# Memory attention of the prompt: scores from two row halves into a bank per head, in place of padded keys

## The chip, the cores and the metric

One Trainium2 chip, and one of its cores. The time is the device time of one execution in microseconds (us): the median of three runs. The profile is of one execution more, taken by the hardware profiler. TensorE has two sequencer streams in it: PE are its matmuls, PEld the loads of its stationary operand. DVE is VectorE, ACT is ScalarE, POOL is GpSimd, and SP is SyncE, which issues most of the DMAs.

## The reference, cut to what matters

The program is one step of a decoder layer, for a prompt of 4096 tokens and for 8 sequences of 4 new tokens. All branches read one projection of the normalized input, 12 blocks of 256 columns. The branch of this change is the cross-attention of the prompt's tokens into 256 memory tokens, with 4 heads of 64:

```
mk, mv = jnp.split(mem @ w, 2, axis=-1)                   # (1, 256, 4, 64) each
def mem_attend(q, mk, mv):
    s = jnp.einsum("nlhd,nmhd->nhlm", q, mk) * (64 ** -0.5)
    p = jax.nn.softmax(s, axis=-1)
    return jnp.einsum("nhlm,nmhd->nlhd", p, mv)
```

Its result is normalized, gated and multiplied with the output projection together with the other three branches (a state space model, a short convolution, and a stick-breaking attention).

## The kernel before, in words

The program has two stages. The first (tile pools `sb1` and `ps1`, up to about 1960 us) goes through the prompt in 8 chunks of 512 tokens. For each chunk it multiplies 24 column blocks of 128 with the chunk's input (`proj`, lines 218 to 220: three fp32r matmuls of 512 columns for each of 8 slices, into the tile `pj`). After each quarter or half of a block, `between` and `slot` let other work into the order: they step generators in the list `bg` (memory attention, state space model, transposed stores, merges) and the decode's generator. This is an order written out by hand, and each engine runs its instructions in it. The second stage (lines 1380 and on) does the prompt's stick-breaking attention (`scores`, line 1449, tile `z`) and the output projection.

The memory attention of a chunk is `mem_gen`, once for each pair of heads (`hp`), so 16 times in all. It takes the four tiles of 128 tokens in two halves. `score` makes the scores of one tile of tokens: one fp32 matmul (line 789) whose stationary operand is `mq`, the transposed queries of both heads of the pair (64 rows each), and whose moving operand is `mkbd`. This holds the keys of both heads beside each other, 512 columns, with zeros where the rows of one head meet the columns of the other, so that one matmul over 128 rows gives the scores of both heads apart. An fp32 matmul stands in the trace as two passes. The result fills one PSUM bank, the tile `ms_`. VectorE takes the maximum of each head (line 791) and scales it (line 792); ScalarE computes the exponentials (the tile `p`; all activations have line 42) with this as bias. Exp needs another table than the activations around it, so an ACT_TABLE_LOAD stands ahead of the exponentials. `scale` divides by the sums (lines 773 and 775), `turn` transposes the weights (line 781, tile `pT`) and copies them out of PSUM, on VectorE for even tiles of tokens and on ScalarE for odd ones, and `mem_pv` multiplies with the values (line 821, tile `mo`).

Two calls of `score` always stand next to each other: tiles 0 and 1 at the start of `mem_gen`, and tiles 2 and 3 behind `mem_pv` of tile 0. So there are 32 such pairs, called score steps below: 16 first ones and 16 second ones. A second step stands right behind `turn(1)`, whose copy out of PSUM is ScalarE's, and `mem_pv(0)`.

The PSUM tiles of `ms_` come from `trp`, the tag `tr`, which has two banks. All transposes of the first stage share them (`pT`, `xx`, `ub`, `uT`, `yT`, `rt`, `bc`, `nat`, `xT`, `wT`, `cT`, `hT`): they are given out in turn, and the next user of a bank waits until the last instruction that reads the one before has ended. Behind a score step, the next user in the order of the program gets the bank of the step's first tile, and the one after it the other.

No two fp32 matmuls over 64 rows stand beside each other in this kernel. Column tiles are used in fp32 in stage one: lines 821 (64 columns of the array) and 1084 (16 columns, the decode's scores, tile `dz`). In stage two line 1449 multiplies over 64 rows, one head in each half of the array, in fp32r, one head's matmul next to the other's.

Of the kernel before, what the change touches and what calls it, by code (L numbers as in the profile page):

```python
# [8 lines left out]
F32 = mybir.dt.float32  # L9
F32R = mybir.dt.float32r  # L10
I32 = mybir.dt.int32
AF = mybir.ActivationFunctionType
ALU = mybir.AluOpType
AX = mybir.AxisListType
# [15 lines left out]
def hymba_kernel(ctx: ExitStack, tc: tile.TileContext, x_p, x_s, cache_k, cache_v, s_re, s_im, s_conv,  # L30
# [7 lines left out]
    mm, tr = nc.tensor.matmul, nc.tensor.transpose  # L38
    V, S, P, SP = nc.vector, nc.scalar, nc.gpsimd, nc.sync

    def act(out, in_, f=AF.Copy, **kw):
        return S.activation(out, in_, f, **kw)  # L42
# [68 lines left out]
    sb = p1.enter_context(tc.tile_pool(name="sb1", bufs=1))  # L111
# [3 lines left out]
    def ev(dt=F32, name="ev"):  # L115
        return sb.tile([128, 512], dt, tag="ev", name=name, bufs=5)

    def m4(name, shape=(128, 2, 512)):
        return sb.tile(list(shape), F32, tag="m4", name=name, bufs=5)

    def m8(name, shape=(128, 2, 1024)):
        return sb.tile(list(shape), F32, tag="m8", name=name, bufs=1)

    def trp(name="trp"):
        return ps.tile([128, 4, 128], F32, tag="tr", name=name, bufs=2)

    def msp(name="msp"):
        return ps.tile([128, 512], F32, tag="ms", name=name, bufs=2)
# [54 lines left out]
    def x_tile(name="xt", dt=F32):  # L183
        return sx.tile([128, DM], dt, tag="xt", name=name, bufs=4)
# [532 lines left out]
            yield  # L717


    mkbd = sb.tile([128, 2, 2, 256], F32, name="mkbd")  # L720
    mv = sb.tile([128, 2, GW], F32, name="mv")

    def mem_setup():
        mT = m8("mT", (128, KT, 256))
        xts, wms = [], {}
        for i in range(2):
            xts.append(x_tile())
            SP.dma_start(xts[i], mem_p[0, i * 128:(i + 1) * 128, :])

        def wm_load(cc):  # L730
            if cc < 4:
                wms[cc] = m4("wm", (128, KT, 128))
                SP.dma_start(wms[cc], w_mem[cc])
        V.memset(mkbd, 0.0)
        wm_load(0)
        wm_load(1)
        yield
        for i in range(2):
            for k4 in range(2):
                t = trp("mTp")  # L740
                for k in range(4):
                    tr(t[:, k, :], xts[i][:, (k4 * 4 + k) * 128:(k4 * 4 + k + 1) * 128], ident)
                V.tensor_copy(mT[:, k4 * 4:k4 * 4 + 4, i * 128:(i + 1) * 128], t)
            yield
        mk = m4("mk", (128, 2, 2, 256))
        for cc in range(4):
            wm = wms.pop(cc)
            wm_load(cc + 2)
            o = msp("mo")
            for i in range(2):  # L750
                for k in range(KT):
                    mm(o[:, i * 128:(i + 1) * 128], mT[:, k, i * 128:(i + 1) * 128], wm[:, k, :],
                       start=(k == 0), stop=(k == KT - 1))
            V.tensor_copy(mk[:, cc // 2, :, cc % 2 * 128:cc % 2 * 128 + 128],
                          o[:, 0:256].rearrange("p (i f) -> p i f", i=2))
            yield
        V.tensor_copy(mv, mk[:, 1])
        SP.dma_start(o_mk[0, 0].rearrange("(i p) h d -> p i (h d)", p=128), mk[:, 0])
        SP.dma_start(o_mv[0, 0].rearrange("(i p) h d -> p i (h d)", p=128), mk[:, 1])
        t = trp("mkT")  # L760
        for hp in range(2):
            for i in range(2):
                tr(t[:, 2 * hp + i, :], mk[:, 0, i, hp * 128:(hp + 1) * 128], ident)
        for hp in range(2):
            for h in range(2):
                V.tensor_copy(mkbd[h * 64:h * 64 + 64, hp, h, :].rearrange("p (i m) -> p i m", i=2),
                              t[h * 64:h * 64 + 64, 2 * hp:2 * hp + 2, :])

    def mem_gen(mq, Y, hp):
        pts, mxs = [], []  # L770

        def scale(t):
            V.reciprocal(mxs[t][:, 6:8], mxs[t][:, 4:6])
            for h in range(2):
                V.tensor_scalar(pts[t][:, h, :], pts[t][:, h, :], mxs[t][:, 6 + h:7 + h], None, op0=ALU.mult)

        def turn(t):
            tp = trp("pT")
            for h in range(2):
                for m in range(2):  # L780
                    tr(tp[:, 2 * h + m, :], pts[t][:, h, m * 128:(m + 1) * 128], ident)
            pT = ev()
            (act if t % 2 else V.tensor_copy)(pT, tp.rearrange("p a b -> p (a b)"))
            return pT

        def score(t):
            s = trp("ms_")
            s2 = s.rearrange("p a b -> p (a b)")
            mm(s2, mq[:, t * 128:(t + 1) * 128], mkbd[:, hp].rearrange("p h m -> p (h m)"), start=True, stop=True)
            mx = sb.tile([128, 8], F32, tag="mx", name="mx", bufs=4)  # L790
            V.tensor_reduce(mx[:, 0:2], s2.rearrange("p (h m) -> p h m", h=2), axis=AX.X, op=ALU.max)
            V.tensor_scalar(mx[:, 2:4], mx[:, 0:2], -0.125, None, op0=ALU.mult)
            p = sb.tile([128, 2, 256], F32, tag="q4", name="p", bufs=4)
            for h in range(2):
                act(p[:, h, :], s2[:, h * 256:(h + 1) * 256], AF.Exp, scale=0.125, bias=mx[:, 2 + h:3 + h],
                    accum_out=mx[:, 4 + h:5 + h])
            pts.append(p)
            mxs.append(mx)
        score(0)
        score(1)  # L800
        yield
        o = msp("mo")
        for t in (0, 2):
            scale(t)
            scale(t + 1)
            yield
            pT = turn(t)
            yield
            pT2 = turn(t + 1)
            mem_pv(o, pT, t, hp)  # L810
            if t == 0:
                score(2)
                score(3)
            yield
            mem_pv(o, pT2, t + 1, hp)
        act(Y[:, hp, :], o)

    def mem_pv(o, pT, t, hp):
        for m in range(2):
            for h in range(2):  # L820
                mm(o[h * 64:h * 64 + 64, t * 128:(t + 1) * 128],
                   mv[:, m, (2 * hp + h) * 64:(2 * hp + h) * 64 + 64],
                   pT[:, (2 * h + m) * 128:(2 * h + m) * 128 + 128], start=(m == 0), stop=(m == 1))
# [383 lines left out]
    def post(i):  # L1207
# [25 lines left out]
        elif blk == M_Q:  # L1233
            mq = sb.tile([128, 512], F32, tag="mq", name="mq", bufs=2)
            act(mq, o)
            if ft == 0:
# [4 lines left out]
                st["mem"] = []  # L1241
                bg.append(chain(st["mem"]))
            st["mem"].append(mem_gen(mq, st["Ym"], ft))
        elif blk == B_C:
            conv_c(o, ft, c)
# [48 lines left out]
    bg.append(dec_consts())  # L1294
    setup = ssm_setup()
    mset = mem_setup()

    def first():
# [8 lines left out]
    i = 0  # L1307
    while i < len(seq):
        c, k = divmod(i, npc)
# [58 lines left out]
    sb = ctx.enter_context(tc.tile_pool(name="sb2", bufs=1, reuse_waits="tile"))  # L1368
# [505 lines left out]
    for i in range(nu + LAG + 1):  # L1874
        j = i - LAG
        z = None
        if i < nu:
            qc, hp, kb, qt = units[i]
# [64 lines left out]
```

## Time and profile before

| | us |
|---|---|
| median of 3 runs | 3415.83 |
| lowest and highest run | 3399.83, 3421.22 |
| profiled execution | 3414.53 |
| its span, first to last instruction | 3412.8 |
| mean granted TensorE clock | 0.973 of full speed |

The profiled execution is 1.3 us below the median. The trace has PE busy in 93% of the span, DVE in 67%, ACT in 52% and POOL in 37%. A busy PE is not PE at its peak, since a matmul's record holds its latency too: what it costs in a row of matmuls is read from start to start.

### The profile page before, as it was taken

How to read it: one execution, taken by the hardware profiler on the slowest of the kernel's cores; microseconds unless marked ns; L12 is line 12 of the kernel's file. 1: busy time of each engine (PE TensorE's matmuls, PEld its weight loads, DVE VectorE, ACT ScalarE, POOL GpSimd, SP SyncE). 2: the span in 40 equal slices, each digit the busy share in tenths (PEclk: the TensorE clock that was granted, in tenths of full speed). 3: DMA queues.
4: the chain of work that ended last, by engine and by line, in shares of the span. 5: the costliest groups of instructions: out<-in, count | busy, mean ns of one | idle time of the engine just before them, and what ended most of it. 6: DMA issues, size and time to landing. Idle time of an engine off the chain costs nothing. (4 is left out here: it accounts for less than half of the span.)

```text
span 3412.8 us, 65273 instructions
## 1 busy us (share of the span) xinstructions
PE 3164.8 (93%) x23383; PEld 2282.1 (67%) x23383; DVE 2283.0 (67%) x3628; ACT 1780.8 (52%) x3324; POOL 1267.6 (37%) x1721
## 2 busy tenths in 40 slices
PE   7888999999999999999999988998999888999998
PEld 6556767667677677676676655666666555666667
DVE  5875667666676676676756566667666777677773
ACT  3435544443444444444434366666656666667771
POOL 1465322222231122222222045555545445555560
PEclk9899999999999999999999979999999999999999
DMA  6677887888877878878887443232323223222223
GB/s 212 194 209 224 279 268 238 264 279 274 267 251 254 286 245 290 263 234 277 270 262 214 142 163 103 91 97 87 97 87 95 71 91 102 94 86 75 88 66 117
DMA packets 382179, 623.57 MB, mean 183 GB/s; under 512 B 54568, under 2 KB 245488, under 8 KB 381856
## 3 DMA queue, kind: packets, MB, share of 16 engines
q1 hardware_dynamic: 344912, 484.90, 45.1%
q0 software_dynamic: 36944, 134.50, 11.9%
q8 instruction: 186, 3.05, 0.4%
q14 instruction: 137, 1.12, 0.1%
HBM read 539.33 MB, written 79.95 MB: 181 GB/s over the span
## 5 line engine op out<-in xcount | busy, mean ns | idle before, releaser
L45 POOL TENSOR_TENSOR bt<-bt,T 128x512 f32<-128x512 f32 (+3 forms) x576 | 605.9, 1052 | 632.2 <-DVE T L1470 417.0
L218 PE MATMUL pj<-xh,whl 128*128 128x512 f32 (+1 forms) x1792 | 724.9, 405 | 0.0
L1470 DVE TENSOR_TENSOR_SCAN T<-om,cy,z 128x513 f32<-128x513 f32 x448 | 549.7, 1268 | 249.3 <-ACT bt L42 96.6
L220 PE MATMUL pj<-xh,whl 128*128 128x512 f32 (+1 forms) x1792 | 658.7, 368 | 9.4 <-DVE whl L45 9.4
L219 PE MATMUL pj<-xh,whl 128*128 128x512 f32 (+1 forms) x1792 | 658.2, 367 | 0.1
L888 POOL DMA_INDIRECT kt<-in_cache_sb_k_dram,idxk x256 | 298.4, 1166 | 898.5 <-DVE kT L1056 787.0
L42 ACT ACTIVATE wT<-wt 128x512 f32<-128x512 f32 (+3 forms) x360 | 194.5, 556 | 448.8 <-PE wt L1487 448.2
L218 PEld LDWEIGHTS pj<-xh,whl 128*128 128x128 f32 x1792 | 344.3, 192 | 120.2 <-issue 82.0
L220 PEld LDWEIGHTS pj<-xh,whl 128*128 128x128 f32 x1792 | 344.0, 192 | 70.3 <-DVE whl L45 12.3
L42 ACT ACTIVATE bt<-z,b 128x512 f32<-128x512 f32 (+3 forms) x576 | 385.2, 669 | 0.0
L42 ACT ACTIVATE om<-z,nb 128x512 f32<-128x512 f32 (+3 forms) x576 | 380.4, 660 | 2.8 <-PE z L1453 2.8
L219 PEld LDWEIGHTS pj<-xh,whl 128*128 128x128 f32 x1792 | 345.6, 193 | 44.9 <-issue 8.6
L1487 PE MATMUL wt<-ident,bt 128*128 128x128 f32 x2112 | 299.5, 281 | 35.2 <-DVE Yc L45 13.5
L1056 DVE STREAM_TRANSPOSE kT<-kt 128x1024 f32<-128x1024 f32 x256 | 315.3, 1232 | 14.9 <-DMA kt<-in_cache_sb_k_dram,idxk 10.3
L1449 PE MATMUL z<-kst,qst 64*128 64x512 f32 (+3 forms) x1704 | 300.1, 424 | 24.2 <-DVE T L1470 21.7
L1487 PEld LDWEIGHTS wt<-ident,bt 128*128 128x128 f32 x2112 | 241.4, 143 | 105.4 <-issue 59.0
L45 DVE TENSOR_TENSOR whl<-stg,whl 128x1024 fp32r<-128x1024 f32 x191 | 234.1, 1226 | 109.3 <-ACT whl L42 99.0
L1503 PE MATMUL ya<-wT,vt 128*64 128x256 f32 (+1 forms) x2176 | 262.8, 382 | 0.3 <-DVE wT L1490 0.3
L42 ACT ACTIVATE whl<-stg 128x1024 fp32r<-128x1024 f32 x192 | 203.1, 1058 | 85.7 <-issue 36.6
L1449 PEld LDWEIGHTS z<-kst,qst 64*128 64x128 f32 x1704 | 152.3, 191 | 129.8 <-issue 52.2
L1560 PE MATMUL wo<-wo,mt 128*128 128x512 f32 x512 | 221.4, 432 | 2.3 <-ACT mt L42 2.3
L1562 PE MATMUL wo<-wo,mt 128*128 128x512 f32 x512 | 206.5, 403 | 0.5 <-DVE mt L45 0.5
(756 smaller groups left out, 4890.5 us busy)
## 6 DMA issues: line engine op xcount, KB each, us to landing
vt<-in_cache_sb_v_dram SPq DMA_DIRECT2D x1024, 128.0 KB
stg<-in_w_in_dram SPq DMA_DIRECT2D x192, 512.0 KB
kst<-kscr SPq DMA_DIRECT2D x71, 512.0 KB
xt<-in_x_prompt_dram SPq DMA_DIRECT2D x64, 512.0 KB
pkt<-pack_d SPq DMA_DIRECT2D x64, 449.0 KB
vt<-vscr SPq DMA_DIRECT2D x71, 256.0 KB
mr<-mscr SPq DMA_DIRECT2D x32, 512.0 KB
out_dram<-yb SPq DMA_DIRECT2D x32, 512.0 KB
```

The lines of the kernel that those rows point to most:

```text
L42: return S.activation(out, in_, f, **kw)
L45: return eng.tensor_tensor(out=out, in0=a, in1=b, op=op)
L218: mm(o[:, t0:t1], hi[:, k, :], xh[:, k, 0, t0:t1], start=(k == 0), stop=False)
L219: mm(o[:, t0:t1], hi[:, k, :], xh[:, k, 1, t0:t1], start=False, stop=False)
L220: mm(o[:, t0:t1], lo[:, k, :], xh[:, k, 0, t0:t1], start=False, stop=(k == KT - 1))
L888: P.indirect_dma_start(out=kq[j], out_offset=None, in_=ck_rows, in_offset=bass.IndirectOffsetOnAxis(ap=idxk[:, u // NU, gg:gg + 1], axis=0))
L1056: V.transpose(kts[j], kq.pop(j))
L1449: mm(zs[h][:, 0:n], qs[r, lq_, qt * 128:(qt + 1) * 128], ks[r, lk, 0:n], start=(lq_ + lk == 0), stop=(lq_ == 1 and not diag))
L1470: V.tensor_tensor_scan(T[:, 0:n + 1][:, ::-1], om[:, 0:n + 1][:, ::-1], z[:, 0:1].to_broadcast([128, n + 1]), 1.0 if diag else c, op0=ALU. ...
L1487: tr(t[:, k, :], ws[h][:, k * 128:(k + 1) * 128], ident)
L1503: mm(ya[0][h * 64:h * 64 + 64, q0 * 128:(qt + 1) * 128], v[:, k, h * 64:h * 64 + 64], wTs[h][:, k, q0 - qt + 1:2, :].rearrange("p a b -> p ...
L1560: mm(o, mt[:, k, 0, :], wo[:, k, 0, cs], start=(k == 0), stop=False)
```

## The change

The padded keys go. `mkT` holds the transposed keys of a pair of heads, one head in each half of the partitions, 256 columns. `score` now does a whole step, two tiles of tokens: it takes both banks first, one for each head, and issues four matmuls over 64 rows with 256 moving columns, with the heads alternating. The bank of a head holds the scores of both tiles of tokens, side by side. Two reductions follow, one for each bank, then one multiplication with -0.125 for all four columns, and then the four exponentials, token tile by token tile, with the heads alternating. The reciprocals of a step are one instruction. `turn` and `mem_pv` are as they were.

```diff
-    mkbd = sb.tile([128, 2, 2, 256], F32, name="mkbd")
+    mkT = sb.tile([128, 2, 256], F32, name="mkT")
...
-        V.memset(mkbd, 0.0)
...
         for hp in range(2):
-            for h in range(2):
-                V.tensor_copy(mkbd[h * 64:h * 64 + 64, hp, h, :].rearrange("p (i m) -> p i m", i=2),
-                              t[h * 64:h * 64 + 64, 2 * hp:2 * hp + 2, :])
+            V.tensor_copy(mkT[:, hp].rearrange("p (i m) -> p i m", i=2), t[:, 2 * hp:2 * hp + 2, :])
...
         def scale(t):
-            V.reciprocal(mxs[t][:, 6:8], mxs[t][:, 4:6])
-            for h in range(2):
-                V.tensor_scalar(pts[t][:, h, :], pts[t][:, h, :], mxs[t][:, 6 + h:7 + h], None, op0=ALU.mult)
+            mx = mxs[t]
+            V.reciprocal(mx[:, 12:16], mx[:, 8:12])
+            for t_ in (t, t + 1):
+                for h in range(2):
+                    c = 12 + 2 * h + t_ % 2
+                    V.tensor_scalar(pts[t_][:, h, :], pts[t_][:, h, :], mx[:, c:c + 1], None, op0=ALU.mult)
...
         def score(t):
-            s = trp("ms_")
-            s2 = s.rearrange("p a b -> p (a b)")
-            mm(s2, mq[:, t * 128:(t + 1) * 128], mkbd[:, hp].rearrange("p h m -> p (h m)"), start=True, stop=True)
-            mx = sb.tile([128, 8], F32, tag="mx", name="mx", bufs=4)
-            V.tensor_reduce(mx[:, 0:2], s2.rearrange("p (h m) -> p h m", h=2), axis=AX.X, op=ALU.max)
-            V.tensor_scalar(mx[:, 2:4], mx[:, 0:2], -0.125, None, op0=ALU.mult)
-            p = sb.tile([128, 2, 256], F32, tag="q4", name="p", bufs=4)
+            ss = [trp("ms_").rearrange("p a b -> p (a b)") for h in range(2)]
+            for t_ in range(2):
+                for h in range(2):
+                    r = slice(64 * h, 64 * h + 64)
+                    mm(ss[h][:, t_ * 256:t_ * 256 + 256], mq[r, (t + t_) * 128:(t + t_ + 1) * 128], mkT[r, hp],
+                       start=True, stop=True)
+            mx = sb.tile([128, 16], F32, tag="mx", name="mx", bufs=2)
             for h in range(2):
-                act(p[:, h, :], s2[:, h * 256:(h + 1) * 256], AF.Exp, scale=0.125, bias=mx[:, 2 + h:3 + h],
-                    accum_out=mx[:, 4 + h:5 + h])
-            pts.append(p)
-            mxs.append(mx)
+                V.tensor_reduce(mx[:, 2 * h:2 * h + 2], ss[h].rearrange("p (t m) -> p t m", t=2), axis=AX.X, op=ALU.max)
+            V.tensor_scalar(mx[:, 4:8], mx[:, 0:4], -0.125, None, op0=ALU.mult)
+            for t_ in range(2):
+                p = sb.tile([128, 2, 256], F32, tag="q4", name="p", bufs=4)
+                for h in range(2):
+                    c = 2 * h + t_
+                    act(p[:, h, :], ss[h][:, t_ * 256:t_ * 256 + 256], AF.Exp, scale=0.125, bias=mx[:, 4 + c:5 + c],
+                        accum_out=mx[:, 8 + c:9 + c])
+                pts.append(p)
+            mxs[t] = mx
         score(0)
-        score(1)
...
             scale(t)
-            scale(t + 1)
...
             if t == 0:
                 score(2)
-                score(3)
```

## Rows read from the trace of the kernel before

**Rows 1.** The page's first part, busy time of each engine, its share of the span and its instructions; and the busy time in one of three like stretches of stage one (start and end, length, then PE, PEld, DVE, ACT, POOL with their instructions, the granted clock, the share of the DMA engines, GB/s).

```profile
PE 3164.8 (93%) x23383; PEld 2282.1 (67%) x23383; DVE 2283.0 (67%) x3628; ACT 1780.8 (52%) x3324; POOL 1267.6 (37%) x1721
...
500.00:1000.00 500.00, 485.92 (x4030) 359.12 (x4028) 339.80 (x576) 227.99 (x438) 121.10 (x155) 0.99 0.81 264
```

**Rows 2.** The timeline of TensorE around the score step at 1156.79 us (start, duration, engine, line and operation, tiles, shapes, number of passes; in brackets the idle time before and what ended it).

```profile
1156.79 1.13 PE L789 MATMUL ms__14119<-mkbd,mq 128*128 128x512 f32 x2
1157.75 1.02 PE L789 MATMUL ms__14127<-mkbd,mq 128*128 128x512 f32 x2
...
1158.61 0.19 PEld L219 LDWEIGHTS pj<-xh,whl 128*128 128x128 f32 x1 [0.24 <-issue]
```

**Rows 3.** TensorE's timeline where tiles of the array are used beside each other, and plain matmuls of 512 columns for comparison: two of the projection, the six of a step of line 1449 and what follows them, and the sixteen passes of the decode's scores and what follows them.

```profile
1160.93 0.39 PE L219 MATMUL pj<-xh,whl 128*128 128x512 f32 x1
1161.16 0.39 PE L220 MATMUL pj<-xh,whl 128*128 128x512 f32 x1
...
2500.15 0.96 PE L1449 MATMUL z<-kst,qst 64*128 64x512 f32 x6
2501.05 0.33 PE L1487 MATMUL wt<-ident,bt 128*128 128x128 f32 x1
...
387.20 0.63 PE L1084 MATMUL dz<-kT,qbd 128*16 128x128 f32 x16
387.65 1.05 PE L1095 MATMUL dO<-vt,dwT 128*16 128x256 f32 x16
```

**Rows 4.** The timelines of VectorE, ScalarE and TensorE behind the same score step, up to the next user of its first bank.

```profile
1157.95 0.69 DVE L791 TENSOR_REDUCE mx<-ms__14119 128x2 f32<-128x512 f32 x1 [2.28 <-PE ms__14119 L789]
1158.67 0.17 DVE L792 TENSOR_SCALAR mx<-mx 128x2 f32<-128x2 f32 x1
1158.81 0.69 DVE L791 TENSOR_REDUCE mx<-ms__14127 128x2 f32<-128x512 f32 x1
...
1158.92 1.28 ACT L42 ACT_TABLE_LOAD   x1 [1.42 <-DVE mx L792]
1160.22 0.48 ACT L42 ACTIVATE p<-ms__14119,mx 128x256 f32<-128x256 f32 x1
...
1161.13 0.47 ACT L42 ACTIVATE p<-ms__14127,mx 128x256 f32<-128x256 f32 x1
...
1161.29 0.35 PEld L330 LDWEIGHTS nat<-ident,ev 128*128 128x128 f32 x3 [0.17 <-ACT p L42]
1161.39 0.38 PE L330 MATMUL nat<-ident,ev 128*128 128x128 f32 x2
```

**Rows 5.** The bank that a second score step takes last: ScalarE's copy of `pT` out of it and TensorE's load that waits for it, in the step that starts at 1123.38 us (rows 6), and the same copy in the step that starts at 956.47 us.

```profile
1123.63 0.58 ACT L42 ACTIVATE ev<-pT 128x512 f32<-128x512 f32 x1
1124.26 0.30 PEld L789 LDWEIGHTS ms__13743<-mkbd,mq 128*128 128x128 f32 x2 [0.58 <-ACT ev L42]
...
955.98 0.60 ACT L42 ACTIVATE ev<-pT 128x512 f32<-128x512 f32 x1 [2.91 <-PE pT L781]
...
956.47 1.12 PE L789 MATMUL ms__11568<-mkbd,mq 128*128 128x512 f32 x2
```

**Rows 6.** TensorE's timeline at score steps and at the next user of their first bank, in the groups of the prediction: the last of those with a late user; the first and the last with a user at some 6.2 us; the first and the last at some 5.4 us; the first and the last at some 4.6 us; and, of the first chunk, the two users that waited for the exponentials.

```profile
1906.73 1.12 PE L789 MATMUL ms__23357<-mkbd,mq 128*128 128x512 f32 x2
...
1916.81 0.38 PE L330 MATMUL nat<-ident,ev 128*128 128x128 f32 x2
...
493.79 1.12 PE L789 MATMUL ms__5768<-mkbd,mq 128*128 128x512 f32 x2
...
500.00 0.39 PE L656 MATMUL xx<-ub,pkt 128*128 128x128 f32 x2
...
1313.96 1.02 PE L789 MATMUL ms__16105<-mkbd,mq 128*128 128x512 f32 x2
...
1320.07 0.39 PE L656 MATMUL xx<-ub,pkt 128*128 128x128 f32 x2
...
460.19 1.12 PE L789 MATMUL ms__5399<-mkbd,mq 128*128 128x512 f32 x2
...
465.75 0.49 PE L623 MATMUL uT<-ident,uf 128*128 128x128 f32 x3
...
1787.28 1.12 PE L789 MATMUL ms__22063<-mkbd,mq 128*128 128x512 f32 x2 [0.43 <-issue]
...
1792.57 0.39 PE L656 MATMUL xx<-ub,pkt 128*128 128x128 f32 x2
...
1123.38 1.13 PE L789 MATMUL ms__13735<-mkbd,mq 128*128 128x512 f32 x2
...
1128.00 0.95 PE L299 MATMUL rt<-sel,ev 128*128 128x1 f32 x8
...
1619.64 1.13 PE L789 MATMUL ms__19919<-mkbd,mq 128*128 128x512 f32 x2
...
1624.25 0.38 PE L330 MATMUL nat<-ident,ev 128*128 128x128 f32 x2
...
127.24 0.33 PE L511 MATMUL cT<-ident,ev 128*128 128x128 f32 x1 [1.67 <-ACT p L42]
...
259.89 0.49 PE L299 MATMUL rt<-sel,ev 128*128 128x1 f32 x3 [4.10 <-ACT p L42]
```

**Rows 7.** The clearing of the padded keys before the first chunk's memory attention (groups of instructions by line and form; busy time and mean ns, idle time before).

```profile
L734 DVE MEMSET mkbd<- 128x1024 f32 x1 | 0.9, 912 | 0.2 <-DVE ev L931 0.2
```

More of the change, by code (lines that the diff above doesn't have):

```diff
@@ L764, in mem_setup @@
         for hp in range(2):
-            for h in range(2):
-                V.tensor_copy(mkbd[h * 64:h * 64 + 64, hp, h, :].rearrange("p (i m) -> p i m", i=2),
-                              t[h * 64:h * 64 + 64, 2 * hp:2 * hp + 2, :])
+            V.tensor_copy(mkT[:, hp].rearrange("p (i m) -> p i m", i=2), t[:, 2 * hp:2 * hp + 2, :])
     def mem_gen(mq, Y, hp):
-        pts, mxs = [], []
+        pts, mxs = [], {}
         def scale(t):
-            V.reciprocal(mxs[t][:, 6:8], mxs[t][:, 4:6])
-            for h in range(2):
-                V.tensor_scalar(pts[t][:, h, :], pts[t][:, h, :], mxs[t][:, 6 + h:7 + h], None, op0=ALU.mult)
+            mx = mxs[t]
[4 more added lines that the diff above has]
+                    V.tensor_scalar(pts[t_][:, h, :], pts[t_][:, h, :], mx[:, c:c + 1], None, op0=ALU.mult)
         def turn(t):
```

## The prediction, made before the change was run

> **What bounds the kernel now.** I read the busy table first: PE is busy in 93% of the span, no other engine in more than 67%. The stretches say where this kernel's change falls: in stage one PE is busy 486 of 500 us at a clock of 0.99, VectorE 340, ScalarE 228 [rows 1]. So TensorE's order sets the time of stage one, a matmul left out there is time won, and an engine's longer work costs only where TensorE then waits for it. Such waits come through the two banks of the tag `tr`. Third, therefore, I followed one score step through the timelines, from TensorE [rows 2] over VectorE and ScalarE to the next user of its first bank [rows 4], and then looked in how many of the 32 steps that user comes soon [rows 6]. All sums are against the profiled execution's own 3414.5 us, 1.3 below the median of the runs.
>
> **TensorE's part of a step.** Before: the second tile's matmul starts 1157.75 - 1156.79 = 0.96 behind the first, and two more passes of 0.43 lie between it and the load of the next matmul but one at 1158.61 [rows 2]. So a step is 0.10 to get in and four passes of 0.43: 1.82 us. After: eight passes of 256 columns, at half of 0.43 each 0.215. If the two heads run beside each other, that is four times 0.215. The nearest rows say that they do. Line 1449's six matmuls of 512 columns, alternating between the halves, take 2501.05 - 2500.15 = 0.90, while one such matmul alone takes 1161.16 - 1160.93 = 0.23, so six would take 1.38; three take 0.69 and the remaining 0.21 is entry and exit [rows 3]. Those are fp32r, one pass each. That two-pass fp32 goes side by side too shows in the decode's scores: sixteen passes in four column tiles take 387.65 - 387.20 = 0.45 [rows 3], a quarter of sixteen passes of 128 columns at 0.107. I take full overlap, with 0.10 at either end, of which the entry was there before: 0.10 + 0.86 + 0.09 = 1.05, so 0.77 us less for a step. The bounds are no overlap, 1.91, and no cost at the exit, 0.96. Over 32 steps the most that can be won is 32 x 0.86 = 27.5 us, 0.8% of the time.
>
> The Trainium skill says in "TensorEngine Tiling (Array Packing)", section Overview, that a contraction of at most 64 rows gains up to two times from row tiles. By that rule alone the sum would be 27.5 us less, 3387; the rows of the banks below make it about nothing.
>
> **The bank that is not free yet.** A second score step follows `turn(1)`, whose tile ScalarE still copies out. Before, only the second matmul needed that bank: its load waited until 1124.26, right behind the copy's end at 1124.21, while the first matmul's 0.96 kept TensorE busy until 1124.34 [rows 2, 5, 6]. After, the second of four matmuls needs it, and the rest stands behind it in order. In that step the copy ends 0.83 after the step's start; head two starts at 0.93 and the step ends at 0.93 + 0.86 + 0.09 = 1.88, so nothing is won (-0.06). In the step at 956.47 the copy ends at 956.58, 0.11 after the start, and 0.65 is won [rows 5, 6]. Of the 16 second steps seven are of the first kind (0.71 to 0.89); in the others the copy ends 0.13 or less after the start, or before it.
>
> **VectorE and ScalarE behind it.** Before, in rows 4: first reduction at 1157.95, multiplication 1158.67, then ScalarE loads the table for Exp (it waits for that multiplication), first exponential at 1160.22, the next at steps of 0.455. The first bank's readers are over with the second exponential, and the next user's load follows at 1161.29, 4.50 after the step's start. After: the first head's bank holds both tiles' scores, filled at 0.10 + 0.86, as early as before. But the one multiplication now stands behind both reductions: 1157.95, 1158.66, multiplication at 1159.38, so 0.71 later, and with it the table load and all exponentials: the first at 1160.93. And the first bank is now read by the third exponential too, 0.91 behind the first, ending at 1162.31; with the 0.14 that lay between exponential and load, the next user starts at 1162.45, 5.65 after the step's start. So the bank comes free 1.15 us later, and TensorE comes to it 0.77 earlier. Where the copy of the last part delays the step, it is 6.05.
>
> **The sum over the 32 steps**, by the time from the step's start to the next user of the bank (call it n; the new time is the larger of n - 0.77, or what is left of the 0.77, and 5.65):
> Late users, n from 6.9 up (the last: 1916.81 - 1906.73 = 10.1): 11 steps, all keep their 0.77 or 0.65, -8.0.
> n about 6.2 (first 500.00 - 493.79, last 1320.07 - 1313.96): 6 steps, five keep 0.57, one nothing, -2.8.
> n from 5.3 to 5.6 (first 465.75 - 460.19, last 1792.57 - 1787.28): 8 steps, 0.1 to 0.4 lost, up to 0.76 where the copy is late, +3.0.
> n about 4.6 (first 1128.00 - 1123.38, last 1624.25 - 1619.64): 4 steps, 1.05 and 1.43 lost, twice each, +5.0.
> The first chunk's three steps whose user already waited for the exponentials (by 1.67 and 4.10 in two of them): they come 0.7 and 0.45 later, +3.3.
> Together -10.8 + 11.3 = +0.5 us [rows 6].
>
> **The rest, costed at nothing.** VectorE loses 32 multiplications of 0.17 [rows 4], as many smaller reciprocals, the memset of 0.9 [rows 7] and two of four copies: it waits for TensorE at a step anyway (2.28 us idle in rows 4) and has 160 of 500 us free [rows 1]; without that cover it would be some 10 us won. The reductions, exponentials, transposes and all DMAs stay in number and order. ScalarE's next work after a step starts 0.7 later; it is mostly the high half of a weight block for TensorE's next block of columns, which no step waits for; without that cover it would be 32 x 0.7 = 22 us at most. SP's and POOL's queues are passed by nothing. Not excluded is that TensorE, let go earlier or later, meets another wait: since gains and losses here are about equal, I take this as plus or minus a few us.
>
> **Rivals.** (a) The gain is kept, as the rule on row tiles has it: the waits at the bank don't come, because the exponentials are not that late (say the reductions start earlier, or the table is loaded already) or because TensorE's wait lets other engines get ahead and is won back at the next wait. Against it: ScalarE's table load waits for the multiplication in rows 4, and TensorE has only 14 us in 500 to win back [rows 1]. It gives the sum without the bank's losses: 18 steps at 0.77, 7 at 0.65 and 7 with nothing or little, -18 us, 3397; with the copy's wait covered too, -25, 3390.
> (b) Slower: the two heads' passes don't run beside each other, because two fp32 passes of one head follow each other before the other head comes. Then a step takes 1.82 + 0.09, nothing is won, and the first head's bank is full 0.43 later, so the exponentials are 1.1 late instead of 0.7. By the same groups: +1.0, +0.9, +6.4, +6.7, +3.3, in all +18 us, 3433. It decides once the overlap is under about half. Against it speak the sixteen passes of rows 3, which are in column tiles though; for it, that no row has fp32 in row tiles. This is also the case in which the change doesn't do what it says.
> (c) Stage one is held by something else than TensorE, DMA at 0.81 of its engines for one [rows 1]; then neither gains nor losses of 1 us show, and the time is that of the forecast.
>
> **Numbers.** The forecast, gains given back at the bank: 0.65, 3414.5 + 0.5, with the 1.3 to the median 3416 us; its own range is 3404 to 3428, from the runs' spread (3400 to 3421) moved by a few us. (a) 0.17, (b) 0.12, (c) goes with the forecast, and 0.06 is left for what I don't see. The range for 8 in 10 reaches into (a) and (b): 3396 to 3432. A measurement of this kernel can tell about 1%, 34 us, from no change. All the cases above stay inside it, since 27.5 us is the most that TensorE can win; so faster by over 1% has 0.06, slower 0.04, within 1% 0.90.
>
> **What would show it.** In the changed kernel's timeline: the score step's eight passes in about 0.95 us, pairs starting together (else b); the first exponential some 4.1 us after the step's start instead of 3.4; idle time of TensorE ended by ScalarE's `p` at `rt`, `nat`, `uT` and `xx` behind the steps, 10 to 14 us in all where it was 6 before, and idle time of half a microsecond within the second steps, ended by the copy of `pT`. PE's busy time in stage one should fall by some 20 us while its span stays. The forecast is wrong if stage one is shorter by more than 10 us, or if those waits are missing.

## The result, and the profile after

The changed kernel takes 3428.5 us (median of 6 runs, 3423.94 to 3437.94) against 3410.4 for the kernel before in the same runs (3399.83 to 3421.22): a ratio of 1.0054, with an interval from 1.0035 to 1.0072. It is 18 us slower: every one of its runs is slower than every run of the kernel before. That is inside the predicted range of 3396 to 3432 and within the 1% for which the prediction had 0.90, but half a microsecond above the range of the forecast itself (3404 to 3428), and not the "about nothing" of its sum. The profiled execution of after, the fastest of the six, has a span of 3422.1 us, 9.3 more than before's.

The page's busy table and the same stretch of stage one, as in [rows 1]:

```profile
PE 3146.9 (92%) x23511; PEld 2278.4 (67%) x23511; DVE 2267.6 (66%) x3561; ACT 1779.9 (52%) x3324; POOL 1266.6 (37%) x1721
...
500.00:1000.00 500.00, 478.89 (x3997) 357.07 (x3996) 330.71 (x550) 227.03 (x438) 120.16 (x152) 0.99 0.81 261
```

TensorE has 17.9 us less work in the whole span (3164.8 - 3146.9), and the span is longer. So TensorE waits more. Stage one as a whole, up to the last matmul of line 220, shows how much. First that matmul and the stretch in the kernel before (stretch, length, PE busy and its instructions, granted clock, DMA share, GB/s):

```profile
1971.01 0.28 PE L220 MATMUL pj<-xh,whl 128*128 128x256 f32 x1
...
100.00:1970.00 1870.00, 1782.78 (x14501) 0.98 0.78 249
```

and in the changed kernel:

```profile
1986.42 0.28 PE L220 MATMUL pj<-xh,whl 128*128 128x256 f32 x1
...
100.00:1985.00 1885.00, 1768.65 (x14620) 0.98 0.77 247
```

Stage one ends 15.4 us later; what follows it, which the change does not touch, is 6.1 us shorter in this profile. So stage one is what is compared below. Busy time in it fell by 14.1 us (1782.78 - 1768.65), idle time rose from 87.2 to 116.4, by 29.1. The granted clock of the stretch is the same, 0.98. The table of what TensorE waited for says where the 29 us lie (engine, tile and line that waited, what released it: us in total, times, longest). In the changed kernel, from 90 to 1985 us:

```profile
PE wT L553 <- DVE wk L45: 10.6, 5, 3.6
PE dz L1088 <- ACT dbt L42: 10.4, 7, 1.8
PE dz L1088 <- DVE kT L1060: 10.2, 10, 2.8
PE nat L330 <- ACT ut L42: 9.9, 3, 3.3
...
PE rt L299 <- ACT p L42: 7.3, 3, 5.2
...
PE nat L330 <- ACT p L42: 2.9, 2, 1.5
```

and in the kernel before, up to the end of its stage one:

```profile
PE wT L553 <- DVE wk L45: 8.6, 5, 2.8
PE nat L330 <- ACT ut L42: 8.5, 3, 2.8
PE dz L1084 <- DVE kT L1056: 7.4, 9, 2.8
...
PE dz L1084 <- ACT dbt L42: 5.9, 7, 1.5
...
PE rt L299 <- ACT p L42: 4.1, 1, 4.1
```

All waits for `p` together went from 5.8 to 18.4 us (with `cT`, `xx`, `wT` and `uT`, which stand further down in that table); those for `dbt` and `ut`, which are later work of ScalarE, from 14.4 to 20.3; those for `kT` by 2.8 and for `wk` by 2.0; and the waits for `ev` inside the second steps, where no matmul waited before, are 6.1. That makes 29 us; what else changed, up and down, is 2 us or less each.

**The step itself.** The step of [rows 2, 4], 1156.79 before, starts at 1165.52 here (TensorE, VectorE and ScalarE):

```profile
1165.52 0.48 PE L792 MATMUL ms__14098<-mkT,mq 64*128 64x256 f32 x1
1165.52 0.48 PE L792 MATMUL ms__14099<-mkT,mq 64*128 64x256 f32 x1
1165.84 0.38 PE L792 MATMUL ms__14098<-mkT,mq 64*128 64x256 f32 x1
1165.84 0.38 PE L792 MATMUL ms__14099<-mkT,mq 64*128 64x256 f32 x1
1166.05 0.38 PE L792 MATMUL ms__14098<-mkT,mq 64*128 64x256 f32 x1
...
1166.92 0.39 PE L219 MATMUL pj<-xh,whl 128*128 128x512 f32 x1
...
1166.68 0.69 DVE L796 TENSOR_REDUCE mx<-ms__14098 128x2 f32<-128x512 f32 x1 [3.18 <-PE ms__14099 L792]
1167.29 0.68 DVE L796 TENSOR_REDUCE mx<-ms__14099 128x2 f32<-128x512 f32 x1
1168.01 0.17 DVE L797 TENSOR_SCALAR mx<-mx 128x4 f32<-128x4 f32 x1
...
1169.55 0.47 ACT L42 ACTIVATE p<-ms__14098,mx 128x256 f32<-128x256 f32 x1
...
1171.08 0.55 PE L330 MATMUL nat<-ident,ev 128*128 128x128 f32 x3 [1.45 <-ACT p L42]
```

In this step the two heads' passes start together, 0.21 us from pair to pair. The second projection matmul behind the step starts 1.40 us after the step's start (1166.92 - 1165.52); before it was 2.05, at 1158.84. So 0.65 us of TensorE's time is saved here. The first exponential starts 4.03 after the step's start (before 3.43), and the next user of the bank 5.56 (before 4.60).

**ScalarE behind it.** At another step ScalarE's work can be followed until TensorE meets it again. Before, from 921.51 (the view is the timeline of TensorE and ScalarE):

```profile
921.51 1.12 PE L789 MATMUL ms__11199<-mkbd,mq 128*128 128x512 f32 x2
923.65 1.28 ACT L42 ACT_TABLE_LOAD   x1 [1.42 <-DVE mx L792]
...
930.25 1.12 ACT L42 ACTIVATE ut<-uT 128x512 f32<-128x512 f32 x2
930.94 1.11 PE L330 MATMUL nat<-ident,ev 128*128 128x128 f32 x4 [2.83 <-ACT ut L42]
```

and the same place in the changed kernel, from 927.08:

```profile
927.08 0.48 PE L792 MATMUL ms__11182<-mkT,mq 64*128 64x256 f32 x1
...
929.82 1.28 ACT L42 ACT_TABLE_LOAD   x1 [2.02 <-DVE mx L797]
931.11 0.47 ACT L42 ACTIVATE p<-ms__11182,mx 128x256 f32<-128x256 f32 x1
...
936.42 1.13 ACT L42 ACTIVATE ut<-uT 128x512 f32<-128x512 f32 x2
937.11 1.12 PE L330 MATMUL nat<-ident,ev 128*128 128x128 f32 x4 [3.30 <-ACT ut L42]
```

Between the table load and `ut` ScalarE pauses nowhere: exponentials, half a weight block, `dwT`, a second table load, `om`, `dbt`, `ut`, one behind the other. So when the first table load waits 2.02 instead of 1.42, everything in this row is 0.60 later, and TensorE, which has to wait for `ut` in both kernels, comes to `nat` 10.03 us after the step's start instead of 9.43. The 0.65 it had saved went into its waits.

**Steps that save nothing.** The 0.65 is not kept in all 32 steps. Read from the trace, step by step: in 13 of the 16 first steps the second head starts 0.05 us or less behind the first, and the second matmul behind the step comes at 1.40 to 1.44 (1.64 in one). In eight second steps the second head starts 0.16 to 0.25 later, and that matmul comes at 1.57 to 1.65, so 0.40 to 0.48 is saved. In the other 11, three first and eight second ones, the bank of the second head comes free only 0.77 us or more after the step's start, and next to nothing is saved, or some is lost. One of them:

```profile
417.74 0.70 PE L792 MATMUL ms__4879<-mkT,mq 64*128 64x256 f32 x2
418.61 0.48 PE L792 MATMUL ms__4880<-mkT,mq 64*128 64x256 f32 x1 [0.18 <-ACT ev L42]
...
420.01 0.39 PE L219 MATMUL pj<-xh,whl 128*128 128x512 f32 x1
```

The pause is 0.18 us only, but the first head's two passes ran alone until then, so the second projection matmul comes 2.27 after the step's start; before it was 2.07. Added up, the steps that overlap save some 12 us (an estimate from these distances), not 32 x 0.65 = 20.8.

Three second steps pause for longer, 3.2, 1.5 and 1.0 us, and one in the first chunk 0.8, for VectorE's `ktl`. The longest, on TensorE and ScalarE:

```profile
661.10 0.70 PE L792 MATMUL ms__7870<-mkT,mq 64*128 64x256 f32 x2
664.99 0.48 PE L792 MATMUL ms__7871<-mkT,mq 64*128 64x256 f32 x1 [3.20 <-ACT ev L42]
...
663.82 0.63 ACT L42 ACTIVATE ev<-ev 128x512 fp32r<-128x512 f32 x1 [3.04 <-DMA qscr<-ev]
664.36 0.58 ACT L42 ACTIVATE ev<-pT 128x512 f32<-128x512 f32 x1
```

ScalarE waits until the store of q has read an `ev` buffer, and the copy of `pT` that frees the bank stands behind that wait.

### The profile page after: what moved, and what is told of

Read it like the earlier page. It is cut to its first block, busy times and chain, and to the rows that moved or that the text cites. A ratio compares the mean times of both kernels' runs of the same rounds, so it can differ in the third digit from the quotient of the medians.

```text
span 3422.1 us, 65416 instructions
## 1 busy us (share of the span) xinstructions
PE 3146.9 (92%) x23511; PEld 2278.4 (67%) x23511; DVE 2267.6 (66%) x3561; ACT 1779.9 (52%) x3324; POOL 1266.6 (37%) x1721
```

## The experiments

My theory after this reading: the loss comes from the one multiplication behind both reductions, through ScalarE's table load and all that follows it. The rivals were the bank (held by the third exponential), the pauses in the second steps, and the row tiles themselves. The first four runs start from the changed kernel, and each takes one of these away.

**e1: one multiplication behind each reduction.**

```diff
             for h in range(2):
                 V.tensor_reduce(mx[:, 2 * h:2 * h + 2], ss[h].rearrange("p (t m) -> p t m", t=2), axis=AX.X, op=ALU.max)
-            V.tensor_scalar(mx[:, 4:8], mx[:, 0:4], -0.125, None, op0=ALU.mult)
+                V.tensor_scalar(mx[:, 4 + 2 * h:6 + 2 * h], mx[:, 2 * h:2 * h + 2], -0.125, None, op0=ALU.mult)
```

> Changed kernel with one multiplication behind each reduction in place of one for both; exponentials in the same order. Theory (the loss comes from ScalarE being let go 0.6 us later in each step and from the bank that its third exponential still reads): the first exponential comes 3.4 us after the step's start instead of 4.0, the bank is free at some 5.0 instead of 5.6, the waits of TensorE for the exponentials and for the decode's sigmoids shrink; 8 to 12 us faster than the changed kernel, ratio to before about 1.002. Rival (the row tiles themselves or chance in the DMAs cost the time, ScalarE is not involved): as the changed kernel, ratio 1.005.

3410.29 us against 3408.42, 1.0011 [0.9998 to 1.0025]. The loss is gone with this one edit; the row tiles' gain does not appear in its place. The waits for `p` fell to 11.0 us, those for `dbt` only to 8.9: the first exponential comes 3.44 us after the step's start, as in the kernel before, and TensorE, which is ahead, waits for the row longer. In stage one it is busy 16 us less than before, at a granted clock of 0.99 instead of 0.98, and idle 15 us more.

**e2: the exponentials head by head**, so that the first bank is free after two of them again; one multiplication as in the changed kernel.

```diff
-            for t_ in range(2):
-                p = sb.tile([128, 2, 256], F32, tag="q4", name="p", bufs=4)
-                for h in range(2):
+            ps2 = [sb.tile([128, 2, 256], F32, tag="q4", name="p", bufs=4) for t_ in range(2)]
+            for h in range(2):
+                for t_ in range(2):
```

> Changed kernel with the exponentials head by head, so that the first bank is free after two of them; still one multiplication. Theory: the first exponential stays at 4.0 us after the step's start, the first bank is free at 5.1 instead of 5.6, ScalarE's later work as late as in the changed kernel; about 6 us faster than the changed kernel, ratio about 1.0035. Rival (only ScalarE's delay counts, not the bank): ratio 1.005. Rival (row tiles or DMAs): 1.005.

3434.03 us against 3408.42, 1.0084 [1.0064 to 1.0104]. The waits for `p` were nearly halved, to 9.8 us, and the time did not fall. So the bank, on which my prediction had put its whole sum, is not what costs the time. That it came out no better, or even a little worse, is not explained by the waits. Stage one of its profile, from 100 us to its last matmul of line 220, shows what it is made of: against the changed kernel's, TensorE is idle 3.7 us less (112.6 against 116.4 us) and busy 8.4 us more (1778.45 against 1770.07) with the same matmuls, at a lower granted clock (0.972 against 0.976 over the span). Why the clock was at its lower level more often stays open.

**e3: both edits.**

> Both: one multiplication for each head, exponentials head by head, so the first bank is free after two exponentials that start at 3.4 us, as in the kernel before. Theory: 12 to 18 us faster than the changed kernel, ratio 0.999 to 1.002; TensorE's waits for the exponentials fall to about the 6 us of before. Rival (row tiles or DMAs): 1.005.

3413.06 us against 3408.42, 1.0014 [1.0004 to 1.0025]: the same as e1 alone, so the order of the exponentials adds nothing here either.

**e4: both turns of a second step ahead of the `yield`**, so that ScalarE's copy of `pT` comes earlier than the second step.

```diff
             pT = turn(t)
-            yield
             pT2 = turn(t + 1)
+            yield
             mem_pv(o, pT, t, hp)
```

> Changed kernel with both turns of a half in one step, ahead of the yield, so that the bank of the second transpose has been copied out long before the second score step; the rest as changed. Theory: the pauses within second score steps (in all some 10 us in the changed kernel's profile, with 0.9 us of steps won back in each) go, minus what the bank of the exponentials then takes back: 4 to 10 us faster than the changed kernel, ratio 1.002 to 1.004. Rival (those pauses came from stores that landed late by chance): no difference in the other steps, ratio 1.005.

3436.55 us against 3408.42, 1.0087 [1.0071 to 1.0104]. The pauses within the second steps are gone, but for one of 1.5 us in the first chunk. Yet `turn` now comes so early in the first chunk that TensorE waits there for other things (waits of TensorE up to 300 us):

```profile
PE rt L299 <- ACT p L42: 8.9, 1, 8.9
...
PE pT L781 <- DVE ktl L559: 5.3, 1, 5.3
```

In the changed kernel the first was 5.2 and the second does not occur. So the run doesn't say what the pauses alone are worth; only that this way of removing them costs more than it brings.

The next two start from both kernels, to have the parts one by one.

**e5: the kernel before, with the one multiplication behind both reductions** (and the one reciprocal of a step, which e1 keeps too); padded keys, one bank for each tile of tokens, and the order of the exponentials stay.

```diff
+            for t_ in range(2):
+                V.tensor_reduce(mx[:, 2 * t_:2 * t_ + 2], ss[t_].rearrange("p (h m) -> p h m", h=2), axis=AX.X, op=ALU.max)
+            V.tensor_scalar(mx[:, 4:8], mx[:, 0:4], -0.125, None, op0=ALU.mult)
```

> Kernel before with one part of the change alone: a step's two reductions first, then one multiplication for both tiles, then the four exponentials; padded keys, a bank for each tile, and TensorE's work as before. Theory, as it stands after e1 to e4 (ScalarE's chain behind a step, table load, exponentials and what is queued behind them, sets the time there, and starts 0.7 us later): most of the change's loss, 10 to 20 us slower than before, ratio 1.003 to 1.006. Rival (the bank for each head or the row tiles make the loss): no difference, 1.000.

3436.5 us against 3408.84, 1.0088 [1.0073 to 1.0103]. This edit alone makes more than the whole loss, 28 us, and more than I expected. One reason shows in its trace: with padded keys the second bank is full later than with row tiles, so the one multiplication delays the row by more. The first exponential comes 4.29 us after the step's start (3.43 before, 4.03 in the changed kernel), at the place of 921.51:

```profile
928.69 1.13 PE L792 MATMUL ms__11157<-mkbd,mq 128*128 128x512 f32 x2
...
932.98 0.47 ACT L42 ACTIVATE p<-ms__11157,mx 128x256 f32<-128x256 f32 x1
```

That is 0.86 later than before, and 32 x 0.86 = 28 us. The waits on the later links of ScalarE's row are as in the changed kernel:

```profile
PE dz L1088 <- ACT dbt L42: 11.1, 7, 1.9
PE nat L330 <- ACT ut L42: 9.9, 3, 3.3
```

**e6: the changed kernel without the row tiles**: padded keys again, a bank for each head, eight passes of 256 columns over 128 rows.

```diff
-                    mm(ss[h][:, t_ * 256:t_ * 256 + 256], mq[r, (t + t_) * 128:(t + t_ + 1) * 128], mkT[r, hp],
+                    mm(ss[h][:, t_ * 256:t_ * 256 + 256], mq[:, (t + t_) * 128:(t + t_ + 1) * 128], mkbd[:, hp, h],
```

> Changed kernel without row tiles: the zero padded keys again, 256 columns over 128 rows for each head and tile, into a bank for each head; all behind TensorE as in the changed kernel. Theory: eight passes of 0.215 behind each other, the first head's bank full at 1.4 us after the step's start instead of 0.96, so ScalarE's chain starts 0.4 later once more and steps with late users lose their 0.65: 10 to 16 us slower than the changed kernel, ratio 1.008 to 1.010. Rival (the row tiles' mode costs as much as it wins): as the changed kernel, 1.005.

3446.02 us against 3408.84, 1.0119 [1.0103 to 1.0136], more than expected. The changed kernel is at 1.0054, so the row tiles do bring 0.65% (1.0119 - 1.0054, some 0.25 either way), some 22 us, against eight passes one behind the other. That is not TensorE's time alone: the first exponential comes 4.47 us after the step's start here, 0.44 later than in the changed kernel.

The last four move ScalarE's table load ahead of the reductions. An exponential of a constant column, whose result is thrown away, is put ahead of each step's first reduction; it waits for nothing of the step, and the table load comes with it. This is additional work of 0.20 us of ScalarE per step.

```diff
+            act(edum, nhalf[:, 0:1], AF.Exp)
             mx = sb.tile([128, 16], F32, tag="mx", name="mx", bufs=2)
```

**e7: the kernel before with it.**

> Kernel before with one exponential of a constant column (thrown away) on ScalarE ahead of each step, so that the table for Exp is loaded while the step's scores and reductions run. Theory: the first exponential comes some 1.3 us earlier (2.1 instead of 3.4 us after the step's start) and with it all of ScalarE's chain; TensorE's waits for p, dbt, ut and ub behind the steps shrink; 5 to 15 us faster than before, ratio 0.996 to 0.998. Rival (ScalarE's start is not what counts): 1.000, or slower by the 32 added instructions' 0.2 us.

3392.93 us against 3408.84, 0.9955 [0.9941 to 0.9970]: faster than the kernel before by 16 us. The place of 921.51, here:

```profile
910.87 1.13 PE L790 MATMUL ms__11215<-mkbd,mq 128*128 128x512 f32 x2
...
911.59 1.28 ACT L42 ACT_TABLE_LOAD   x1
912.88 0.20 ACT L42 ACTIVATE edum<-nhalf 128x1 f32<-128x1 f32 x1
913.02 0.48 ACT L42 ACTIVATE p<-ms__11215,mx 128x256 f32<-128x256 f32 x1
...
918.33 1.12 ACT L42 ACTIVATE ut<-uT 128x512 f32<-128x512 f32 x2
...
919.02 0.66 PE L330 MATMUL nat<-ident,ev 128*128 128x128 f32 x4 [1.55 <-ACT ut L42]
```

The table is loaded while TensorE still computes scores, the first exponential starts 2.15 after the step's start instead of 3.43, `ut` and with it `nat` (8.15 instead of 9.43) come 1.28 earlier, as much as a table load takes. The waits for `dbt` in stage one fell from 5.9 to 1.7 us, for `ut` from 8.5 to 4.7. Stage one of this profile is 21.5 us shorter: TensorE is idle 12.0 us less, and the same matmuls take 9.5 us less, with the granted clock of the stretch at 0.99 instead of 0.98.

**e8: e3 (row tiles, two multiplications, head by head) with it.**

> Changed kernel with a multiplication for each head, exponentials head by head, and the thrown away exponential ahead of each step. Theory: ScalarE's chain starts some 1.3 us earlier than before the change, so that TensorE keeps its 0.65 in nearly all steps and meets fewer waits behind them: 20 to 30 us faster than before, ratio 0.991 to 0.994, and faster than e7. Rival (TensorE's gain is lost to something else than ScalarE): as e7.

3390.97 us against 3408.84, 0.9949 [0.9934 to 0.9965]. It beats both kernels and has the lowest median, but e7, without row tiles, ran beside it and is as fast within the intervals. I had expected the row tiles to show now; they don't. In stage one TensorE is busy 6.1 us less than in e7 and idle 7.6 us more. In 11 of its 32 steps the second head still starts 0.5 us or more behind the first, so they save little or nothing.

**e9: the changed kernel with it, and nothing else.** This puts the theory to the test: if the multiplication hurts only through the start of ScalarE's row, an earlier table load must make up for it.

> Changed kernel as it is, with only the thrown away exponential ahead of each step. Theory (what counts is when ScalarE's chain behind a step starts, not which part of the change delays it): the first exponential comes some 2.8 us after the step's start, earlier than the 3.4 of the kernel before although the one multiplication still stands behind both reductions: 15 to 20 us faster than the changed kernel, ratio to before 0.997 to 1.000. Rival (the one multiplication hurts in another way, on VectorE): 1.003 or more.

3396.6 us against 3407.49, 0.9975 [0.9964 to 0.9986]. The first exponential comes 2.76 us after the step's start, and the ratio is the one that the theory gave; against the changed kernel's 1.0054 it is some 27 us, more than the 15 to 20 that I had said. Its waits:

```profile
PE nat L330 <- ACT ut L42: 8.4, 3, 2.8
...
PE dz L1090 <- ACT dbt L42: 4.9, 7, 1.7
...
PE rt L299 <- ACT p L42: 4.0, 1, 4.0
```

**e10: e8 with the second step moved behind the second half of the products with v**, so that no copy of `pT` can be in its way.

```diff
+                yield
+                mem_pv(o, pT2, 1, hp)
                 score(2)
-            yield
-            mem_pv(o, pT2, t + 1, hp)
```

> e8 with the second score step moved one generator step later, behind mem_pv of tile 1, and the last two turns together in one step, so that no score step meets a bank that is still being copied. Theory: the pauses within second steps (in e8's profile some 0.6 us in most, 2.1 in one) are gone, 3 to 8 us faster than e8, ratio 0.992 to 0.994. Rival (what those steps win is taken back by the next wait for ScalarE, as in e4): as e8, 0.995.

3401.74 us against 3407.49, 0.9982 [0.9970 to 0.9994]: not faster than e8 but slower. A pause taken out of the second step is no gain by itself: in its trace the two heads start together in all second steps, TensorE is busy 13.5 us less than in e8's stage one (1754.63 against 1768.12) and idle 13.8 us more, and stage one ends at the same time (1951.26 and 1950.99).

**The parts, read together.** From before, one multiplication: +0.88% (e5). Banks for each head with eight passes one behind the other on top of it: +0.31% (e6 less e5, an interval of some 0.2 either way). Row tiles in place of those passes: -0.65%. These add up to the change, +0.54%, because each step is measured from the one before it. Taking the multiplication's delay out of the changed kernel gives 0.43% back (e1), not 0.88: there it is 0.59 us (4.03 less 3.44), not 0.86. The runs in the order of the first exponential (us after the step's start, median of the 32 steps in each trace):

| run | row tiles | first exponential | ratio to before |
|---|---|---|---|
| e6 | no | 4.47 | 1.0119 |
| e5 | no | 4.29 | 1.0088 |
| changed kernel | yes | 4.03 | 1.0054 |
| e1, e3 | yes | 3.44 | 1.0011, 1.0014 |
| kernel before | no | 3.43 | 1 |
| e9 | yes | 2.76 | 0.9975 |
| e7 | no | 2.20 | 0.9955 |
| e8 | yes | 2.16 | 0.9949 |

With row tiles or without, the time follows the start of ScalarE's row. A start later than in the kernel before costs nearly its whole delay in each of 32 steps (28 us in e5); an earlier one wins less than half of it (32 x 1.23 = 39 us in e7, of which 16 are measured). The other three lie 0.3% above those with the same start: e2 and e4 (4.03, 1.0084 and 1.0087) and e10 (2.16, 0.9982).

## Why the prediction was right and wrong

**Right: TensorE's part.** The overlap was forecast at 0.77 us for a step and is 0.65; the difference is the exit, costed at 0.09 and measured at 0.21 (0.10 + 0.86 + 0.21 makes the 1.17 by which the saving is 0.65). That holds where both banks are free; 11 of the 32 steps save next to nothing, so it is some 12 us in all. The busy time of stage one fell by 14.1 us, where the prediction had said some 20. Rival (b), no overlap, falls with the pairs that start together, although its 3433 is nearer to the 3428.5 than the forecast's 3416. The rule of the Trainium skill, "TensorEngine Tiling (Array Packing)", section Overview (up to two times), holds for the passes, which come at half their former distance (0.21 us for a pair of 256 columns each, 0.43 for a pass of 512). The 3387 that I had worked out by it does not hold for the kernel, which measures 3428.5.

**Right: the delay of the exponentials.** Forecast 4.14 after the step's start, measured 4.03; next user of the bank forecast 5.65, measured 5.56; waits for `p` forecast at 10 to 14 us in all, measured 18.4, so somewhat more.

**Wrong: the step that failed.** The prediction said of ScalarE: "its next work after a step starts 0.7 later; it is mostly the high half of a weight block for TensorE's next block of columns, which no step waits for", and gave it no price, with 22 us as the most it could cost without that cover. Behind this stands its first paragraph, by which TensorE's waits come through the two banks of `tr`. The cover was not there. The weight block is one link in a row of ScalarE's work without pauses, and behind it stand `dbt`, `ut` and the copies to which TensorE comes soon. The kernel before already waited 14.4 us for `dbt` and `ut` in stage one; its table of waits shows this, and the prediction used that table only for `p`. In the changed kernel the delay is 0.60 us, 32 x 0.60 = 19 us, and the loss is 18; e5 measured it at 28 us in the kernel before, where the delay is 0.86. So it was paid nearly in full. e9 and e7 show that it works through the start of ScalarE's row, since an earlier table load takes it away in the one and gains in the other. That 3428.5 still lies in the range of 3396 to 3432 is luck as far as this term goes: the range was that wide for the rivals' sake, not for ScalarE's row.

**Wrong: the bank.** I let the whole result hang on when the bank comes free. e2 frees it earlier, halves the waits for `p` and gains nothing, and neither does e3 over e1. This fits the row tiles too, which bring nothing in e1 against the kernel before and in e8 against e7: the first exponential comes no earlier by them (3.44 and 3.43, 2.16 and 2.20), as the first bank is full 0.96 us after the step's start in both kernels. Where one multiplication waits for both banks they do let it start earlier (4.03 against 4.29 in e5), and there the ratio is lower with them.

**Right in kind, too small in size: the second steps.** I had seven of them saving nothing, the second head starting at 0.93. Those seven save nothing: in four the second head starts at 0.77 to 0.94, with pauses of some 0.2 where I had said half a microsecond, and in three at 1.66, 2.24 and 3.89, with pauses of 1.0 to 3.2. What I had not seen is the wait in front of the copy, ScalarE's for q's store, and the one step of the first chunk and three first steps whose second bank is late as well. e4 and e10 removed pauses and gained nothing, so I can't say what they cost alone.

**Rival (a)**, the gain kept, gave 3397, and e9 comes to 3396.6, but not by its mechanism: e7, which has no row tiles, gains at least as much from the earlier table load alone. Its condition "the table is loaded already" points at what counts, and I had given it as an aside. **Rival (c)**, that something else holds stage one, falls: e7 shortens stage one (its last matmul of line 220 starts at 1949.52 instead of 1971.01) with all transfers as they were.

Still open: why the granted clock is lower in e2; why e10, with 13.5 us less of TensorE's work in stage one than e8, only waits that much more; and what the pauses in the second steps cost alone.

## What to carry to other kernels

When a change delays one small result, look for what the other engine starts from it and follow that engine's row until it pauses; the price is met where the bounding engine next waits for anything in that row, not at the first reader. An existing wait for a late link of the row, as the 14.4 us here for `dbt` and `ut`, says that the cover is already used up there. And where a function's table load stands behind a data wait, an instruction with the same function and no such wait, put ahead, takes the load off the path: here 16 us for one instruction in each step.

## What was not expected of the hardware

The table load waits with the first exponential: it has no operands, but in both kernels it starts only when that exponential's bias is there (923.65 and 929.82 above, each behind `mx`), and takes 1.28 us; a dummy exponential ahead lets it start at once (911.59). The Trainium skill, "ScalarE activation tables: per-element evaluation and per-set limits", section What a function is on this engine, gives 1283 ns for it, which the trace agrees with; the first exponential follows its end by 0.01 us.

Two-pass fp32 matmuls of 64 rows do run beside each other in the two halves of the rows: in the step at 1165.52 the pairs start at most 0.01 us apart and follow each other at 0.21, half of the 0.43 of a pass of 512 columns. Going back to the full array cost 0.21 us there, about twice what line 1449's fp32r matmuls in [rows 3] had suggested.
